# One more of a feed-forward's weight blocks by seven products instead of eight, with its weights loaded earlier

## The chip, the core and the metric

The kernel runs on one core of one Trainium2 chip. The metric is the device time of one execution in microseconds (us). Three runs of the kernel before gave a median of 1127.21 us (1126.88 to 1127.61).

## What is computed

One layer of a streaming encoder for two request groups that share the weights: 512 prompt tokens and 32 sample tokens, 544 columns in all, with 1024 features. The change lies in the first of its three stages, a gated feed-forward with 2816 hidden features:

```python
def swiglu(h, w_gate, w_up, w_down):
    a = jnp.einsum('btd,df->btf', h, w_gate)
    u = jnp.einsum('btd,df->btf', h, w_up)
    return jnp.einsum('btf,fd->btd', jax.nn.silu(a) * u, w_down)

mod = jnp.einsum('bd,de->be', jax.nn.silu(c), w_cond) + b_cond
sh1, sc1, gt1, sh2, sc2, gt2, sh3, sc3, gt3 = jnp.split(mod, 9, axis=-1)
x = post_norm(x, swiglu(modulate(x, sh1, sc1), f1_gate, f1_up, f1_down), 1.0 + gt1, 0.5, ln1_g, ln1_b)
```

The later stages (retention and sparse attention, output projection, second feed-forward) need the other parts of `mod`.

## The kernel before, in words

The 544 columns are worked in two halves of 272. The 22 blocks `f` of 128 hidden features each need a gate and an up product: weight 1024x128 times activation `h` of 1024x272, for both halves.

Every fp32 operand is split into a high and a low float32r part, and a product of 128x128 by 272 columns is three matmuls: high by high, high by low, low by high. So a gate or up product of one half is 24 matmuls, and an ordinary block (`ffn_mm`) is 4 x 24 = 96.

Blocks `f` in the range `SEVEN[0]` go another way (`feed`, `seven`), by a Strassen-like scheme: gate/up and the two halves of the features and of the columns make a 2x2 by 2x2 product, done with seven products of 12 matmuls, 84 in all. For this the kernel needs

- sums of activations, tiles `hs` (`sums[0..7]`), made once by `activation_sums`. For each of k = 0..3, VectorE makes two tiles `la` and `lb` out of `h[k]` and `h[4+k]` (two additions and four subtractions), ScalarE casts them to the high part of `hs`, and VectorE subtracts for the low part. `la` and `lb` are scratch tiles with four buffers in all (`scr`, `bufs=4`).
- sums of raw weights (`weight_sums`: four VectorE operations in place on the raw tiles `wr_g` and `wr_u`), which `split_sums` then splits: ScalarE casts the high part of `wh_s`, VectorE subtracts for the low part.
- the plain gate weights `wh_g` and half of the up weights `wh_u`, split in another way (`negated`): ScalarE casts the high part and writes its negative in the place of the low part, and GpSimd issues a DMA that adds the raw weights from memory to it. The same is done with the ordinary blocks' `wh_w` (`split_w`).

In a block, `seven` has TensorE work in this order: `pC` with `wh_g`, `pA` with `wh_s` and `hs` (the sums 4 to 7), `pB` with `wh_s` and `hs` (the sums 0 to 3), `pA` again, the next block's first `pA`, and so on. ScalarE copies intermediate `pA` out (`snapshot`).

The order of TensorE's instructions is fixed by the program order (`ordered("pe", ...)`), and so is that of SyncE's loads (`ordered("load", ...)`); GpSimd's DMAs all go into one queue. The rest of each engine's order is set by a scheduler, which `pin` holds to program order for the marked instructions. Each engine executes its instructions in order.

Beside this run the modulation pieces (`cond`): 40 loads of 512 KB of `w_cond`, each with two VectorE operations (`ca`), paced by a tick per group of products (a list of gaps).

Of the kernel before, what the change touches and what calls it, by code (L numbers as in the profile page):

```python
# [9 lines left out]
F32 = mybir.dt.float32  # L10
# [21 lines left out]
SEGS = ((((0, HT), 0),), (((HT, TP), 0), ((TP, T), 1)))  # L32
DOWN_G = ((0, 8), (8, 15), (15, 22))
AHEAD = 3
SEVEN = ((5, 17), (4, NF - 1))
WHOLE = (2, 8)


# [1 line left out]
def encoder_layer_kernel(ctx, tc, xT, cT, wc1, w_e, w_cond, b_condT, lnp, w_gu1, w_dn1, w_in, w_out, w_gu2, w_dn2,  # L40
# [51 lines left out]
    def spawn(job):  # L92
        resume(job, now[0] + 1)
# [26 lines left out]
    def fetch_w(src, n, name):  # L120
        raw = wr.tile([P, ND, P], F32, name=f"wr_{name}", tag="wr")
        load(raw[:, :n, :], src)
        return raw
# [37 lines left out]
    def ensure(n):  # L161
        while len(split) < n and stream and stream[0]:
            if not fetched:
                fetch_ahead()
            src, cnt, kw = stream.pop(0)
            split.append(split_w(fetched.pop(0), cnt, "w", src=src, **kw))
# [5 lines left out]
    def queue_w(src, n=ND, **kw):  # L172
        stream.append((src, n, kw))
# [254 lines left out]

    queue_ffn(w_gu1, w_dn1, True)
    for c in range(4):  # L430
        queue_w(w_in[c], lo_eng=nc.gpsimd if c else nc.vector, pool=up)
    for c in [4] + [17 + hh + 4 * j for hh in range(4) for j in range(3)] + [
            5 + c + 4 * j for c in range(4) for j in range(3)] + [29, 30, 31, 32]:
        queue_w(w_in[c], lo_eng=nc.vector if c in (4, 17) else None)
# [103 lines left out]
    for n in range(len(ACC)):  # L538
        catch_up(n, ND)
    ensure(AHEAD)  # L540
    onesr = const.tile([P, P], FR, name="onesr")
    nc.vector.tensor_scalar(onesr, ones, 2.0, None, op0=ALU.mult)

# [22 lines left out]
    def cond(parts, gaps):  # L566
        todo = [(m, d) for m in parts for d in range(ND)]
        ws, accs = [], {}

        def fetch():  # L570
            if len(ws) < len(todo):
                m, d = todo[len(ws)]
                ws.append(up.tile([P, 1024], F32, name=f"wc{m}_{d}", tag="u"))
                load(ws[-1], w_cond[d * P:(d + 1) * P, 1024 * m:1024 * m + 1024])

        fetch()
        yield 1
        fetch()
        yield 2
        for n, (m, d) in enumerate(todo):  # L580
            if d == 0:
                accs[m] = [up.tile([P, 1024], F32, name=f"ca{m}_{r}", tag="u") for r in range(2)]
            fetch()
            for r, acc in enumerate(accs[m]):
                c = cz[:, d, r:r + 1]
                if d == 0:
                    got = nc.vector.tensor_scalar(acc, ws[n], c, None, op0=ALU.mult)
                else:
                    got = nc.vector.scalar_tensor_tensor(acc, ws[n], c, acc, op0=ALU.mult, op1=ALU.add)  # L589
                tc.add_manual_dep(got.ins, last["pe"], NOSYNC, reason="pace")  # L590
            if d == ND - 1:
                spawn(cond_done(m, accs[m]))
            yield gaps[n % len(gaps)]
# [46 lines left out]
    def later(n, job):  # L640
        yield n
        yield from job
# [13 lines left out]
    def activation_sums(h, sums, pace=False):  # L656
        yield 1 if pace else 0
        for k in range(4):
            ta, tb = sums[k], sums[4 + k]
            la, lb = scr("la"), scr("lb")  # L660
            for x, l in ((h[k], la), (h[4 + k], lb)):
                r = nc.vector.tensor_tensor(l, x[:, 0].bitcast(F32), x[:, 1].bitcast(F32), op=ALU.add)
                if pace:
                    tc.add_manual_dep(r.ins, last["pe"], NOSYNC, reason="pace")
            for o, p, q in ((la[:, 0:HT], la[:, HT:T], la[:, 0:HT]), (la[:, HT:T], lb[:, HT:T], la[:, HT:T]),
                            (lb[:, HT:T], lb[:, HT:T], la[:, 0:HT]), (lb[:, 0:HT], lb[:, 0:HT], lb[:, HT:T])):
                nc.vector.tensor_tensor(o, p, q, op=ALU.subtract)
            for x, l in ((ta, la), (tb, lb)):
                nc.scalar.copy(x[:, 0], l)
                nc.vector.tensor_tensor(x[:, 1], l, x[:, 0].bitcast(F32), op=ALU.subtract)  # L670
            yield 2

    def split_hid(dst, src, n):
        if n == 1:
# [1 line left out]
        else:  # L676
            nc.vector.tensor_tensor(dst[:, 1], src, dst[:, 0].bitcast(F32), op=ALU.subtract)

    def feed(h, hid, sums, flat, begun, gu, blocks, whole, lead=None):
        pin = tc.keep_in_program_order  # L680
        LO, HI = slice(0, 4), slice(4, 8)
        raw_g, raw_u, Wg, Wu, Wg2, Wu2 = {}, {}, {}, {}, {}, {}

        def load_gate(f):
            raw_g[f] = fetch_w(gu[f, 0], ND, "g")

        def load_up(f):
            raw_u[f] = up.tile([P, ND, P], F32, name="wr_u", tag="u")
            load(raw_u[f], gu[f, 1])

# [34 lines left out]
        def snapshot(ps, name):  # L725
            s = half_scr(name)
            pin(nc.scalar.copy(s, ps))  # L727
            return s
# [33 lines left out]
        def seven(f):  # L762
            t, u = scr("tnh", [P, 2, HT]), scr("up", [P, 2, HT])
            more = f < last7
            if f + 2 <= last7:
                make_gate(f + 2)
            else:
                ensure(len(split) + 1)
            if f + 3 <= last7:
                load_gate(f + 3)  # L770
            else:
                fetch_ahead()
            if f + 2 <= last7:
                load_up(f + 2)
            C = bank("l", "pC")[:, :HT]
            product(C, Wg[f], 4, h, 4, 0, True, True)
            pin(nc.vector.tensor_tensor(u[:, 0], s1.pop(f), C, op=ALU.add))
            finish_block(0)
            pin(nc.scalar.activation(t[:, 0], u[:, 0], AF.Silu))
            if more:  # L780
                make_up(f + 1, 0)
            tick()
            product(A[f], Wg2[f], 0, sums, 4, 1, False, True)
            s2 = snapshot(A[f], "s2")
            if more:
                weight_sums(f + 1)
                make_up(f + 1, 1)
            finish_block(1)
            B = bank("t", "pB")[:, :HT]
            product(B, Wu2[f], 0, sums, 0, 1, True, True)  # L790
            tick()
            product(A[f], Wu2[f], 4, sums, 0, 0, False, True)
            s4 = snapshot(A[f], "s4")
            pin(nc.vector.tensor_tensor(u[:, 1], s4, B, op=ALU.add))
            if more:
                begin(f + 1)
                split_sums(f + 1, Wg2, raw_g)
                s1[f + 1] = snapshot(A[f + 1], "s1")
            else:
                (lead or first_down)()  # L800
            finish_block(2)
            tick()
            product(A[f], Wg2[f], 4, h, 4, 1, False, True)
            if more:
                split_sums(f + 1, Wu2, raw_u)
            pin(nc.scalar.activation(t[:, 1], A.pop(f), AF.Silu))
            product(B, Wu[f], 0, sums, 4, 0, False, True)
            pin(nc.vector.tensor_tensor(u[:, 0], s2, B, op=ALU.add))
            pending.append((t, u, f))
            if not more:  # L810
                finish_block(0)
            tick()
# [10 lines left out]
        for f in range(2, first7):  # L823
            place(f)
            if f == first7 - 2:
                load_gate(first7)
                load_up(first7)
            if f == first7 - 1:
                load_gate(first7 + 1)
                load_up(first7 + 1)  # L830
                load_gate(first7 + 2)
            st = [None, None], {}
            for which in range(2):
                for i in range(2):
                    ffn_mm(st, h, which, i)
                    if f == first7 - 2 and which == 0:
                        if i == 0:
                            make_gate(first7)
                        else:
                            make_up(first7, 0)  # L840
                            make_up(first7, 1)
                    if f == first7 - 1:
                        if which == 0 and i == 0:
                            make_gate(first7 + 1)
                        if which == 0 and i == 1:
                            weight_sums(first7)
                        if which == 1 and i == 0:
                            split_sums(first7, Wg2, raw_g)
                            split_sums(first7, Wu2, raw_u)
            for i in range(2):  # L850
                ffn_act(st, hid[f] if f < whole else None, i, flat.get(f))
# [13 lines left out]
        for i in range(2):  # L865
            ffn_act(sts[f], hid[f], i)
    flat, following = {}, ([None, None], {})
    spawn(later(4, cond((2, 3, 4, 5, 6), [3] * 4 + [4] * 3 + [6] + [4] * 6 + [4, 3] + [2] * 24)))
    feed(h, hid, sums, flat, None, w_gu1, SEVEN[0], WHOLE[0], lambda: ffn_mm(following, h, 0, 0))
    hid.extend([None] * len(flat))  # L870

    def split_flat():
# [817 lines left out]
```

## Time and profile before

| | us |
|---|---|
| median of three runs | 1127.21 |
| the profiled execution | 1126.96 |
| its span | 1125.2 |
| TensorE busy | 1106.3 (98%) |
| VectorE busy | 855.2 (76%) |
| ScalarE busy | 638.4 (57%) |
| GpSimd busy | 196.0 (17%) |

The profile gives for each engine when an instruction was busy, and for an idle stretch what ended it. TensorE is busy in nearly the whole span: the first blocks of the feed-forward (`gu`) start at 46.65 us, the seven-product blocks run from 82.6 us to 224 us, and the down projection (`dn`) from 269 us to 404 us. A DMA's time is read from its issue to its landing.

### The profile page before, as it was taken

The page shows a single profiled execution, that of the slowest core. Times are in us where ns is not written, and L with a number is a line of the kernel's source. Part 1 is how long each engine was busy: PE and PEld are TensorE (multiplying, and loading weights), DVE is VectorE, ACT ScalarE, POOL GpSimd, SP SyncE. Part 2 cuts the span into 40 slices and gives each one's busy share as a digit, 9 for nine tenths or more (in the row PEclk, how much of TensorE's full clock was granted, in tenths as well). Part 3 has the DMA queues.
Part 4 walks back from the last instruction along what each step waited for, and adds up shares of the span by engine and source line. Part 5 has one row for each costly group of instructions (what it writes and reads, how often), then busy time and mean ns, then how long its engine had stood idle before and what let it go on. Part 6 is the DMA issues. An engine that isn't in the chain of part 4 may idle for free.

```text
span 1125.2 us, 22775 instructions
## 1 busy us (share of the span) xinstructions
PE 1106.3 (98%) x9047; PEld 1075.8 (96%) x9047; DVE 855.2 (76%) x1774; ACT 638.4 (57%) x1121; POOL 196.0 (17%) x217
## 2 busy tenths in 40 slices
PE   8999999999999999999999999999999999999995
PEld 7999999999999999889999899999999999999994
DVE  5778898788868799797899777798798966810416
ACT  3646656754234355865566678656666666653523
POOL 0111111122101303422210101100111111151100
PEclk9999999999999999999999999999999999999998
DMA  9789878996977556644956588843888677578842
GB/s 358 272 237 249 227 191 228 256 259 243 334 201 185 129 218 171 145 118 124 276 112 215 109 269 232 201 172 57 238 212 215 179 187 161 160 205 178 176 73 80
DMA packets 71164, 220.92 MB, mean 196 GB/s; under 512 B 8624, under 2 KB 12848, under 8 KB 71056
## 3 DMA queue, kind: packets, MB, share of 16 engines
q1 hardware_dynamic: 49456, 151.02, 38.2%
q0 software_dynamic: 21456, 68.30, 33.8%
q8 instruction: 71, 1.16, 0.4%
q14 instruction: 37, 0.30, 0.1%
q10 hardware_dynamic: 144, 0.14, 0.0%
HBM read 207.82 MB, written 9.58 MB: 193 GB/s over the span
## 4 chain that ended last, share of the span: by engine, by line
PE 87%; DVE 6%; DMA 4%; ACT 1%; issue 1%; SPq 0%; DVEq 0%; POOL 0%; POOLq 0%; ACTq 0%
PE dn L77 26%; PE in L77 16%; PE pA L77 15%; PE gu L77 10%; PE pB L77 8%; PE pC L77 4%; DMA we_raw<-in_w_e 3%; PE gu_e L77 2%; PE pt L80 1%; PE po L77 1%; PE lg L77 1%; DMA wh_w<-in_w_dn 1%; PE isc L77 1%; PE ro L77 1%; DVE m L1126 1%
## 5 line engine op out<-in xcount | busy, mean ns | idle before, releaser
L77 PE MATMUL dn<-hid,wh_w 128*128 128x272 f32 x2112 | 267.1, 288 | 0.3 <-DMA wh_w<-in_w_dn 0.3
L77 PEld LDWEIGHTS dn<-hid,wh_w 128*128 128x128 f32 x2112 | 265.5, 188 | 0.7 <-DMA wh_w<-in_w_dn 0.5
L77 PE MATMUL in<-h,wh_w 128*128 128x272 f32 x1392 | 186.7, 291 | 0.0
L77 PEld LDWEIGHTS in<-h,wh_w 128*128 128x128 f32 x1392 | 176.6, 188 | 4.9 <-issue 2.9
L131 ACT CAST wh_w<-wr_w 128x1024 fp32r<-128x1024 f32 (+1 forms) x100 | 100.9, 1014 | 99.9 <-PE dn L77 86.5
L77 PE MATMUL gu<-h,wh_w 128*128 128x272 f32 x864 | 109.1, 288 | 0.0
L77 PEld LDWEIGHTS gu<-h,wh_w 128*128 128x128 f32 x864 | 108.5, 188 | 0.0
L589 DVE SCALAR_TENSOR_TENSOR ca<-wc,cz,ca 128x1024 f32<-128x1024 f32 x84 | 107.4, 1298 | 0.0
L77 PE MATMUL pA<-hs,wh_s 128*128 128x272 f32 x744 | 103.7, 288 | 0.7 <-ACT s L727 0.6
L77 PEld LDWEIGHTS pA<-hs,wh_s 128*128 128x128 f32 x744 | 96.8, 188 | 1.1 <-ACT s L727 1.1
L138 ACT ACTIVATE wh_w<-wh_w 128x1024 fp32r<-128x1024 f32 (+1 forms) x78 | 79.5, 1022 | 1.5
L286 DVE SCALAR_TENSOR_TENSOR xs<-dn,C,xs 128x272 f32<-128x272 f32 (+2 forms) x24 | 9.0, 403 | 81.6 <-PE dn L77 81.6
L693 POOL DMA_DIRECT2D wh_g<-in_w_gu x31 | 27.0, 871 | 250.0 <-ACT wh_g L692 172.6
L727 ACT COPY s<-pA 128x272 f32<-128x272 f32 x93 | 35.5, 382 | 58.5 <-PE pA L77 57.9
L139 POOL DMA_DIRECT2D wh_w<-in_w_dn x32 | 28.1, 879 | 174.9 <-ACT wh_w L138 141.6
L716 DVE TENSOR_TENSOR wh_s<-wr_g,wh_s 128x1024 fp32r<-128x1024 f32 x31 | 38.0, 1224 | 20.2 <-ACT wh_s L715 20.2
L77 PE MATMUL pA<-h,wh_g 128*128 128x272 f32 x372 | 51.8, 288 | 0.0
L77 PE MATMUL pB<-hs,wh_u 128*128 128x272 f32 x372 | 51.5, 287 | 0.0
L77 PE MATMUL pC<-h,wh_g 128*128 128x272 f32 x372 | 51.5, 287 | 0.0
L77 PE MATMUL pB<-hs,wh_s 128*128 128x272 f32 x372 | 51.4, 287 | 0.0
L77 PE MATMUL pA<-h,wh_s 128*128 128x272 f32 x372 | 51.4, 287 | 0.0
L77 PEld LDWEIGHTS pA<-h,wh_g 128*128 128x128 f32 x372 | 48.7, 188 | 0.0
(331 smaller groups left out, 2048.4 us busy)
## 6 DMA issues: line engine op xcount, KB each, us to landing
wc<-in_w_cond SPq DMA_DIRECT2D x52, 512.0 KB, 6.6
wr_w<-in_w_in SPq DMA_DIRECT2D x33, 512.0 KB, 5.4
wr_g<-in_w_gu SPq DMA_DIRECT2D x31, 512.0 KB, 3.7
wr_u<-in_w_gu SPq DMA_DIRECT2D x31, 512.0 KB, 4.5
wh_g<-in_w_gu POOLq DMA_DIRECT2D x31, 512.0 KB, 6.7
wr_w<-in_w_dn SPq DMA_DIRECT2D x32, 448.0 KB, 4.3
wh_w<-in_w_in POOLq DMA_DIRECT2D x27, 512.0 KB, 6.4
wh_w<-in_w_dn POOLq DMA_DIRECT2D x26, 448.0 KB, 6.7
```

The lines of the kernel that those rows point to most:

```text
L77: ordered("pe", nc.tensor.matmul(*a, **kw))
L80: ordered("pe", nc.tensor.transpose(*a))
L131: c = nc.scalar.copy(hi[:, :n, :], raw[:, :n, :])
L138: nc.scalar.mul(lo[:, :n, :], hi[:, :n, :].bitcast(F32), -1.0)
L139: nc.gpsimd.dma_start(lo[:, :n, :], src, accum_op=ALU.add)
L286: nc.vector.scalar_tensor_tensor(x[:, sa:sb], ps[:, sa - a:sb - a], coef[r][:, d:d + 1], x[:, sa:sb], op0=ALU.mult, op1=ALU.add)
L589: got = nc.vector.scalar_tensor_tensor(acc, ws[n], c, acc, op0=ALU.mult, op1=ALU.add)
L693: nc.gpsimd.dma_start(lo, src, accum_op=ALU.add)
L716: pin(nc.vector.tensor_tensor(W[f][:, 1], raw[f], W[f][:, 0].bitcast(F32), op=ALU.subtract))
L727: pin(nc.scalar.copy(s, ps))
L1126: behind(behind(nc.vector.max(m8, w), "pe"), "norm")
```

## The change

- `SEVEN[0]` begins at block 4 instead of 5: fourteen blocks go by seven products, and only blocks 2 and 3 stand as ordinary ones ahead of them.
- The raw gate and up weights of block 4 are loaded ahead of the blocks, right behind the first three weight loads, into tiles of the pool `up`.
- `activation_sums` yields one tick instead of two between its four parts, and for k = 0 and 1 makes the low part of `hs` by a negation on ScalarE and an adding DMA of GpSimd, which reads `la` or `lb`, instead of by VectorE.
- The modulation pieces start five ticks later (`later(9, ...)`), and some of their later gaps are one tick instead of two.
- In `seven`, the first `Silu` stands behind the copy `s2` and the second product instead of ahead of them.
- The second gate of the range is made one product later (`which == 1`).
- Three weights of the input projection, used at about 404 us, have their low part made by negation and an adding DMA instead of by a GpSimd subtraction.

```diff
-SEVEN = ((5, 17), (4, NF - 1))
+SEVEN = ((4, 17), (4, NF - 1))
...
-        queue_w(w_in[c], lo_eng=nc.gpsimd if c else nc.vector, pool=up)
+        queue_w(w_in[c], lo_eng=None if c else nc.vector, pool=up)
...
     ensure(AHEAD)
+    first_raw = ({}, {})
+    for which in range(2):
+        raw = up.tile([P, ND, P], F32, name=("wr_g", "wr_u")[which], tag="u")
+        load(raw, w_gu1[SEVEN[0][0], which])
+        first_raw[which][SEVEN[0][0]] = raw
...
                 nc.scalar.copy(x[:, 0], l)
-                nc.vector.tensor_tensor(x[:, 1], l, x[:, 0].bitcast(F32), op=ALU.subtract)
-            yield 2
+                if pace and k < 2:
+                    nc.scalar.mul(x[:, 1], x[:, 0].bitcast(F32), -1.0)
+                    nc.gpsimd.dma_start(x[:, 1], l, accum_op=ALU.add)
+                else:
+                    nc.vector.tensor_tensor(x[:, 1], l, x[:, 0].bitcast(F32), op=ALU.subtract)
+            yield 1 if pace else 2
...
             finish_block(0)
-            pin(nc.scalar.activation(t[:, 0], u[:, 0], AF.Silu))
             if more:
                 make_up(f + 1, 0)
             tick()
             product(A[f], Wg2[f], 0, sums, 4, 1, False, True)
             s2 = snapshot(A[f], "s2")
+            pin(nc.scalar.activation(t[:, 0], u[:, 0], AF.Silu))
...
-                        if which == 0 and i == 0:
+                        if which == 1 and i == 0:
                             make_gate(first7 + 1)
...
-    spawn(later(4, cond((2, 3, 4, 5, 6), [3] * 4 + [4] * 3 + [6] + [4] * 6 + [4, 3] + [2] * 24)))
-    feed(h, hid, sums, flat, None, w_gu1, SEVEN[0], WHOLE[0], lambda: ffn_mm(following, h, 0, 0))
+    spawn(later(9, cond((2, 3, 4, 5, 6), [3] * 4 + [4] * 3 + [6] + [4] * 6 + [4, 3] + [2] * 10 + [2, 1] * 5 + [2] * 4)))
+    feed(h, hid, sums, flat, None, w_gu1, SEVEN[0], WHOLE[0], lambda: ffn_mm(following, h, 0, 0),
+         first_raw)
```

The first place is GpSimd's queue at the start of the feed-forward. `wh_w` are low parts of ordinary blocks, `wh_g` and `wh_u` those of seven-product blocks, and the wait of a row is the semaphore of another engine or of a DMA. Before, behind the subtraction:

```order
L141 TENSOR_TENSOR wh_w<-wr_w,wh_w 128x1024 [waits DMAHW4_49,Activation_49]
L139 DMA wh_w<-in_w_gu 128x1024 [waits Activation_49] x3
L139 DMA wh_w<-in_w_gu 128x1024 [waits PE_49,Activation_49,Pool_49]
L693 DMA wh_g<-in_w_gu 128x1024 [waits DVE_49,PE_49,Activation_49]
L693 DMA wh_u<-in_w_gu 128x512 [waits DMAHW1_49,Activation_49]
```

The same place in the changed kernel:

```order
L141 TENSOR_TENSOR wh_w<-wr_w,wh_w 128x1024 [waits DMAHW4_49,Activation_49]
L139 DMA wh_w<-in_w_gu 128x1024 [waits Activation_49] x2
L708 DMA wh_g<-in_w_gu 128x1024 [waits Activation_49]
L677 DMA hs<-la 128x544 [waits DVE_49,PE_49,Activation_49]
L677 DMA hs<-lb 128x544 [waits DVE_49,DMAHW5_49,PE_49,Activation_49]
L708 DMA wh_u<-in_w_gu 128x512 [waits DMAHW0_49,PE_49,Activation_49]
L677 DMA hs<-la 128x544 [waits DVE_49,DMAHW1_49,PE_49,Activation_49]
L677 DMA hs<-lb 128x544 [waits DMAHW2_49,DMAHW6_49,DVE_49,Activation_49]
```

Three adding DMAs of 512 KB stand first in both kernels. Behind them the queue now holds four adding DMAs of `hs` with 128x544 elements (272 KB) and, between them, one of 256 KB for `wh_u`. The semaphores of GpSimd's DMAs go round eight numbers in this order, so the first `hs<-la` is DMASW3, the first `hs<-lb` DMASW4 and the second `hs<-la` DMASW6.

The second place is VectorE at the sums of k = 2 and k = 3 (`h_2`, `h_6` and `h_3`, `h_7`), where `flat` is the activation of block 2 and `gu` its products. Before:

```order
L662 TENSOR_TENSOR la<-h_2_94 128x544
L662 TENSOR_TENSOR lb<-h_6_98 128x544
L667 TENSOR_TENSOR la<-la 128x272 [waits DVE_49]
L667 TENSOR_TENSOR la<-lb,la 128x272 [waits DVE_49]
L667 TENSOR_TENSOR lb<-lb,la 128x272 [waits DVE_49]
L667 TENSOR_TENSOR lb<-lb 128x272 [waits DVE_49]
L670 TENSOR_TENSOR hs<-la,hs 128x544 [waits DMAHW4_49,Activation_49]
```

In the changed kernel:

```order
L667 TENSOR_TENSOR la<-h_2_94 128x544 [waits DMASW3_49,Activation_49]
L672 TENSOR_TENSOR la<-la 128x272 [waits DVE_49]
L667 TENSOR_TENSOR lb<-h_6_98 128x544 [waits DMASW4_49,Activation_49]
L672 TENSOR_TENSOR la<-lb,la 128x272 [waits DVE_49]
L672 TENSOR_TENSOR lb<-lb,la 128x272 [waits DVE_49]
L672 TENSOR_TENSOR lb<-lb 128x272 [waits DVE_49]
L679 TENSOR_TENSOR hs<-la,hs 128x544 [waits DMAHW4_49,Activation_49]
L203 TENSOR_TENSOR flat<-tnh,gu_0_777 128x272 [waits DMAHW0_49,PE_49]
L679 TENSOR_TENSOR hs<-lb,hs 128x544 [waits Activation_49]
L203 TENSOR_TENSOR flat<-tnh,gu_1_816 128x272 [waits PE_49]
L667 TENSOR_TENSOR la<-h_3_95 128x544 [waits DMASW6_49]
L667 TENSOR_TENSOR lb<-h_7_99 128x544 [waits DVE_49]
```

The third `la` and `lb` now wait for the first two adding DMAs of `hs`, whose source buffers they overwrite, and the fourth `la` waits for the third of those DMAs. Before, none of these rows waited for a DMA of GpSimd.

The third place is VectorE between those sums and the first seven-product block, 4 (`wr_g` and `wr_u` are its raw weights, `gu` the up products of block 3, `pC` the block's own product), in the changed kernel:

```order
L679 TENSOR_TENSOR hs<-lb,hs 128x544 [waits DMAHW4_49,Activation_49]
L726 TENSOR_TENSOR wr_u<-wr_u 128x512 [waits DMAHW0_49]
L203 TENSOR_TENSOR flat<-tnh,gu_0_931 128x272 [waits PE_49]
L726 TENSOR_TENSOR wr_u<-wr_g,wr_u 128x512 [waits DMAHW7_49,DVE_49]
L726 TENSOR_TENSOR wr_g<-wr_u,wr_g 128x512 [waits DVE_49,Pool_49]
L726 TENSOR_TENSOR wr_g<-wr_g 128x512 [waits DVE_49]
L203 TENSOR_TENSOR flat<-tnh,gu_1_966 128x272 [waits PE_49]
L731 TENSOR_TENSOR wh_s<-wr_g,wh_s 128x1024 [waits Activation_49]
L731 TENSOR_TENSOR wh_s<-wr_u,wh_s 128x1024 [waits DMASW0_49,Activation_49]
L792 TENSOR_TENSOR up<-s_1010,pC 128x272 [waits DMASW7_49,PE_49,Activation_49]
```

The corresponding rows before, ahead of block 5, with the pieces of the modulation (`ca`) among them:

```order
L711 TENSOR_TENSOR wr_u<-wr_g,wr_u 128x512 [waits DMAHW1_49]
L587 TENSOR_SCALAR ca_0_983<-wc_0_872,cz 128x1024 [waits DMAHW4_49,DMAHW0_49]
L670 TENSOR_TENSOR hs<-lb,hs 128x544 [waits Activation_49]
L587 TENSOR_SCALAR ca_1_984<-wc_0_872,cz 128x1024
L711 TENSOR_TENSOR wr_g<-wr_u,wr_g 128x512 [waits DVE_49]
L711 TENSOR_TENSOR wr_g<-wr_g 128x512 [waits DVE_49]
```

The pieces of the modulation are gone from this stretch; the weight sums of the first seven-product block stand right behind the last sum of activations.

More of the change, by code (lines that the diff above doesn't have):

```diff
@@ L677, in split_hid, with feed @@
             nc.vector.tensor_tensor(dst[:, 1], src, dst[:, 0].bitcast(F32), op=ALU.subtract)
-    def feed(h, hid, sums, flat, begun, gu, blocks, whole, lead=None):
+    def feed(h, hid, sums, flat, begun, gu, blocks, whole, lead=None, first_raw=({}, {})):
         pin = tc.keep_in_program_order
@@ L682, in feed @@
         raw_g, raw_u, Wg, Wu, Wg2, Wu2 = {}, {}, {}, {}, {}, {}
+        raw_g.update(first_raw[0])
+        raw_u.update(first_raw[1])
         def load_gate(f):
-            raw_g[f] = fetch_w(gu[f, 0], ND, "g")
+            if f not in raw_g:
+                raw_g[f] = fetch_w(gu[f, 0], ND, "g")
         def load_up(f):
+            if f in raw_u:
+                return
             raw_u[f] = up.tile([P, ND, P], F32, name="wr_u", tag="u")
```

## The prediction

> **What bounds the kernel now.** First the page's busy times and the table of who waited for whom on TensorE (us in total, times, longest), for what TensorE has to do and what it waits for.
>
> ```profile
> PE 1106.3 (98%) x9047; PEld 1075.8 (96%) x9047; DVE 855.2 (76%) x1774; ACT 638.4 (57%) x1121; POOL 196.0 (17%) x217
> PE pA L77 <- ACT s L727: 0.6, 1, 0.6
> PE dn L77 <- DMA wh_w<-in_w_dn: 0.3, 1, 0.3
> ```
>
> TensorE works in 98% of the span. In the change's stages it waits only 0.6 us for a ScalarE copy and 0.3 us for a weight. So a matmul less is time less, and any new wait of TensorE is time more. The chain of waits (start, us, what) prices a product: the three ordinary blocks, and 12 matmuls of `pA`.
>
> ```profile
> 46.65 36.08 PE gu L77 x288
> 82.73 1.52 PE pA L77 x12
> ```
>
> 36.08 / 288 = 0.1253 us per matmul; a product of 24 takes 3.01 us, one of 12 takes 1.50.
>
> **One block by seven products.** It saves 96 - 84 = 12 matmuls, 1.5 us on TensorE, which sets the end. The rest of the question is whether what the first seven-product block needs is there a block earlier. With two ordinary blocks ahead, TensorE reaches block 4 at 46.65 + 8 x 3.01 = 70.7 us; after the first `pA` and `pC` it wants `wh_s` and `hs` at 73.7, and the low part of `wh_s`, by the third matmul, at 73.95. Nothing ahead of 46.65 moves: the early raw loads stand behind the loads that these blocks start with, and the DMA engines are idle then. Of the busy time by stretches the last two columns are the share of the 16 DMA engines and the GB/s:
>
> ```profile
> 40.00:44.00 4.00, 3.96 (x31) 3.63 (x30) 2.46 (x5) 3.88 (x6) 2.23 (x1) 1.00 0.03 12
> 46.00:65.00 19.00, 19.00 (x154) 19.00 (x153) 14.80 (x31) 9.91 (x20) 2.76 (x3) 1.00 1.01 292
> ```
>
> From 46 to 65 us, however, the DMA engines are full, and now the sums of activations go through them. Two of the four leave VectorE in favour of adding DMAs, in one queue behind the three adding DMAs of weights. GpSimd's timeline (start, us) shows when those three were issued, and the DMA tables of the stretches 46 to 51, 51 to 53 and 53 to 55 how long each took to land:
>
> ```profile
> 46.58 1.02 POOL L139 DMA_DIRECT2D wh_w<-in_w_gu  x1 [2.39 <-ACT hid L206]
> 51.84 0.87 POOL L139 DMA_DIRECT2D wh_w<-in_w_gu  x1 [4.24 <-ACT wh_w L138]
> 54.00 0.86 POOL L139 DMA_DIRECT2D wh_w<-in_w_gu  x1 [1.29 <-ACT tnh L201]
> wh_w<-in_w_gu POOLq DMA_DIRECT2D x1, 512.0 KB, 10.1
> wh_w<-in_w_gu POOLq DMA_DIRECT2D x1, 512.0 KB, 8.7
> wh_w<-in_w_gu POOLq DMA_DIRECT2D x1, 512.0 KB, 11.3
> ```
>
> They landed at 56.7, 60.5 and 65.3: one per 3.8 to 4.8 us, one behind the other. The changed queue has the same three first, and beside them SyncE still loads weights, only two fewer (those moved ahead), so I keep 65.3 for the third. The first `hs<-la` cannot land before it, though ScalarE casts the first sum already at about 54:
>
> ```profile
> 53.88 0.64 ACT L669 CAST hs<-la 128x544 fp32r<-128x544 f32 x1
> ```
>
> What one of 272 KB takes no row shows. The upper end is 272/512 of the mean spacing above, 4.3 us: 2.3. For the lower, GpSimd's rows of a 512 KB DMA with a 256 KB one behind it, and their tables (86 to 88, 88 to 89):
>
> ```profile
> 87.11 0.88 POOL L693 DMA_DIRECT2D wh_g<-in_w_gu x1 [6.71 <-ACT tnh L779]
> 88.75 0.87 POOL L693 DMA_DIRECT2D wh_u<-in_w_gu x1 [0.75 <-ACT wh_u L692]
> wh_g<-in_w_gu POOLq DMA_DIRECT2D x1, 512.0 KB, 6.8
> wh_u<-in_w_gu POOLq DMA_DIRECT2D x1, 256.0 KB, 6.4
> ```
>
> Landings at 93.9 and 95.15, 1.25 us apart, so 1.3 for 272 KB. I take the middle, 1.85. Then `la` of k = 0 lands at 67.15, `lb` at 69.0, and behind `wh_u` `la` of k = 1 at 72.7.
>
> VectorE, which executes in order, cannot start the third `la` before the first has landed (its buffer), nor the third `lb` before the second. Queued behind these are all sums of k = 2 and 3, the four weight sums and the low part of `wh_s`, for which TensorE waits. Their durations, from VectorE's timeline of k = 1 (two additions, four subtractions, the low parts, `flat`), of a block's weight sums, and of the low part of `wh_s`; and ScalarE's cast ahead of the latter:
>
> ```profile
> 55.84 0.72 DVE L662 TENSOR_TENSOR la<-h 128x544 f32<-128x544 f32 x1
> 57.11 0.43 DVE L667 TENSOR_TENSOR la<-la 128x272 f32<-128x272 f32 x1
> 58.89 0.72 DVE L670 TENSOR_TENSOR hs<-la,hs 128x544 fp32r<-128x544 f32 x1
> 59.52 0.43 DVE L203 TENSOR_TENSOR flat<-tnh,gu 128x272 f32<-128x272 f32 x1
> 59.87 0.72 DVE L670 TENSOR_TENSOR hs<-lb,hs 128x544 fp32r<-128x544 f32 x1
> 99.80 0.69 DVE L711 TENSOR_TENSOR wr_u<-wr_u 128x512 f32<-128x512 f32 x1
> 102.64 0.43 DVE L794 TENSOR_TENSOR up<-s,pB 128x272 f32<-128x272 f32 x1
> 84.33 1.22 DVE L716 TENSOR_TENSOR wh_s<-wr_u,wh_s 128x1024 fp32r<-128x1024 f32 x1
> 79.09 1.04 ACT L715 CAST wh_s<-wr_g 128x1024 fp32r<-128x1024 f32 x1
> ```
>
> From the landing of `lb` to the start of the fourth `la`: an addition 0.63, three subtractions of 0.475, two low parts of 0.63 and two `flat` of 0.35, with 0.1 for the wait: 4.1 us, so 73.1, 0.4 after its own buffer came free. From there: two additions and four subtractions 3.05, two low parts 1.28, the four weight sums 2.84 with one `flat` 0.35 between them, the cast 1.04, the low part 1.22, 0.2 for two handovers: 10.0 us. The low part of `wh_s` is there at 83.1, wanted at 73.95: **TensorE waits 9.1 us**. By the ends 1.3 and 2.3 the fourth `la` starts at 72.1 or 74.6, and the wait is 8.2 or 10.7.
>
> Such a wait costs more than itself. The clock slows when TensorE stands still: its last matmul before the end of the kernel, and the granted clock (third column from the right) behind it; and at the kernel's start the same matmul cold and warm:
>
> ```profile
> 1111.37 0.62 PE L77 MATMUL pv<-sq,cm 128*128 128x272 f32 x2
> 1112.00:1114.00 2.00, 0.00 (x0) 0.00 (x0) 1.89 (x4) 0.68 (x2) 1.67 (x2) 1.00 0.00 0
> 1116.00:1118.00 2.00, 0.00 (x0) 0.00 (x0) 1.91 (x4) 0.70 (x2) 0.00 (x0) 0.50 0.00 0
> 1.23 3.78 PE L77 MATMUL idle<-zeros 128*128 128x256 f32 x8 [1.23 <-POOL zeros L496]
> 7.48 2.76 PE L77 MATMUL idle<-zeros 128*128 128x256 f32 x12
> ```
>
> Between 2 and 6 us after the last matmul the clock is at half, and eight cold matmuls took 3.78 us where warm ones take 8 x 0.23: 1.9 us lost. After a pause of 8 us I expect the same loss, +1.9; its ends are 0 and twice that. The Trainium skill, "TensorE: Matmul & The Clock Gate", section "What's actually happening", has the clock at half after an idle window of about 3.4 us and until a busy one of the same length; by that the loss would be an estimated 1.7 us instead, and the rows agree with the rule. It speaks against this change.
>
> Once through, I expect no second wait: the up weights' `wh_s` follow 1.2 us later, TensorE has 1.5 us of work until then, and each later block brings VectorE its usual work within 10.5 us, without the pieces of the modulation for now.
>
> **The other edits.** The `Silu` behind the copy `s2`: the copy no longer waits in ScalarE's queue for VectorE's sum, so the 0.6 us goes (0 to -0.6; what the `Silu` feeds is wanted a block later). The four negations are ScalarE's, which has room in the 46 to 65 row. The pieces of the modulation start later but end at the same tick, so five of them move towards the down projection, where TensorE hides them (in 46 to 404 us it waits only for the two above); were that cover gone, a piece's two operations cost 2.5 us of VectorE. The input projection's three low parts free GpSimd, where a subtraction stood ahead of the late weight:
>
> ```profile
> 375.00 3.44 POOL L141 TENSOR_TENSOR wu_w<-wr_w,wu_w 128x1024 fp32r<-128x1024 f32 x1 [1.31 <-ACT wu_w L131]
> 378.38 0.88 POOL L139 DMA_DIRECT2D wh_w<-in_w_dn  x1
> ```
>
> That weight's DMA now comes ahead of them: -0.3 (to 0).
>
> **The sum**, against the profiled execution, 1126.96 us (span 1125.2, 1.76 around it; 0.25 under the median): 1126.96 - 1.5 - 0.6 - 0.3 + 9.1 + 1.9 = **1135.6**. With the bounds above its own range is 1132.8 (wait 8.2, no cold clock) to 1140 (wait 10.7, twice the cold loss, the two small gains at nothing).
>
> **Rivals.**
> *The sums come in time: faster.* The first `hs<-la` is ready to be issued at about 55.3. If GpSimd's queue were drained by then, each transfer would land soon after issue, the fourth `la` would start by 63 and `wh_s` be ready by 73. Then nothing stands against the savings: 1126.96 - 2.4 = 1124.6. Against it are the three rows that landed up to 65.3; for it only that two loads move into the idle stretch ahead of 46. It decides from the point at which the first `hs<-la` lands before about 58. 10%. The Trainium skill, "DMA: Bandwidth & Descriptors", section "Anatomy of one DMA", fits an adding queue's transfer by 2.0 us and its bytes at 436 GB/s; that would be an estimated 2.6 us for these 272 KB and would carry this rival. The rows of 10.1, 8.7 and 11.3 us for 512 KB do not agree.
>
> *A shorter wait.* With fewer loads beside them the three land up to 3 us earlier, at 62.3, and the following at 1.3 spacing: `lb` at 64.9, the fourth `la` at 69, `wh_s` at 79, a wait of 5.1, and 1126.96 - 2.4 + 5.1 + 1.9 = 1131.6; between this and the first rival lies all that ends at no change. 15%, 6 of them within 0.2%.
>
> *A longer wait.* If a DMA out of on-chip memory is paid by the row and not by the byte, each `hs` costs 4.3 like 512 KB: the second `la` lands at 65.3 + 3 x 4.3 + 2.2 = 80.4, the wait is 16.5 and the time 1143. No row shows such a source. 7%.
>
> **The numbers.** The forecast has 68%. 0.2% of the time, 2.3 us, is about what a measurement of this kernel can tell from no change. Faster: the first rival, 10%. Same: 6%. Slower: 68 + 9 + 7 = 84%. The range leaves out the first rival, the part at no change and most of the longest wait: 1129.5 to 1140.
>
> **What would show it.** In the changed profile: TensorE idle for about 9 us at 74 us, ahead of `pA<-hs,wh_s`, released by VectorE's `wh_s`; GpSimd's `hs` DMAs issued from 55 and landing after more than 8 us; VectorE idle ahead of the third `la`, released by a DMA; the granted clock under 1 in that slice; 192 matmuls `gu` ahead of the blocks. I am wrong if the first `hs<-la` lands before 60, or if TensorE runs through 74 us.

## The result, and the profile after

| | before | after |
|---|---|---|
| median of the runs, us | 1127.30 (1126.88 to 1127.61, 4 runs) | 1137.58 (1136.63 to 1138.71, 4 runs) |
| profiled execution, us | 1126.96, span 1125.2 | 1138.71, span 1136.9 |
| matmuls on TensorE | 9047 | 9035 |

The ratio is 1.0091 [1.0078, 1.0104]: the changed kernel is slower by 10.3 us (8.8 to 11.7). The page's busy times and the table of who waited for whom on TensorE (us in total, times, longest), of the changed kernel:

```profile
PE 1108.6 (98%) x9035; PEld 1076.8 (95%) x9035; DVE 855.4 (75%) x1778; ACT 647.1 (57%) x1133; POOL 190.5 (17%) x221
...
PE pA L77 <- ACT s L742: 9.1, 1, 9.1
PE pC L77 <- DVE flat L203: 0.4, 1, 0.4
```

The twelve matmuls are gone, yet TensorE is busy for 2.3 us more: some matmuls ran slower. And there is one new wait of 9.1 us. TensorE's timeline (start, us, what, and in brackets the idle time before it with what ended it) shows where:

```profile
73.52 1.77 PE L77 MATMUL pC<-h,wh_g 128*128 128x272 f32 x12 [0.41 <-DVE flat L203]
84.36 3.09 PE L77 MATMUL pA<-hs,wh_s 128*128 128x272 f32 x12 [9.08 <-ACT s L742]
87.25 2.92 PE L77 MATMUL pB<-hs,wh_s 128*128 128x272 f32 x12
89.97 1.83 PE L77 MATMUL pA<-hs,wh_s 128*128 128x272 f32 x12
91.64 1.68 PE L77 MATMUL pA<-h,wh_g 128*128 128x272 f32 x12
```

TensorE ends `pC` at 75.3 and stands until 84.36, ahead of the first product with `hs` and `wh_s`. Then it is slow: the 36 matmuls from 84.36 to 91.64 took 7.28 us, where 36 x 0.1253 is 4.51. So 2.8 us more are lost behind the wait. The busy times by stretches name the reason in their third column from the right, the granted clock:

```profile
78.00:80.00 2.00, 0.00 (x0) 0.00 (x0) 1.92 (x5) 1.97 (x3) 0.00 (x0) 1.00 0.00 0
80.00:82.00 2.00, 0.00 (x0) 0.00 (x0) 1.86 (x4) 0.21 (x1) 0.88 (x1) 0.52 0.00 0
...
88.00:90.00 2.00, 2.00 (x11) 2.00 (x11) 1.69 (x3) 0.72 (x2) 0.86 (x1) 0.50 0.91 143
90.00:92.00 2.00, 2.00 (x16) 2.00 (x16) 0.00 (x0) 0.16 (x1) 0.00 (x0) 0.92 1.03 193
```

The clock is full for almost 5 us after the last matmul, then at half from 80 to a little past 90, nearly 6 us into the new work.

Whom TensorE waits for is read backwards. On GpSimd, the four adding DMAs of `hs` (start of the issue, us), and their landing from the DMA tables of the stretches 57 to 58, 61 to 62, 68 to 69 and 70 to 71 (KB, us from issue to landing):

```profile
57.50 0.89 POOL L677 DMA_DIRECT2D hs<-la  x1 [2.79 <-ACT hs L674]
61.27 0.88 POOL L677 DMA_DIRECT2D hs<-lb  x1 [2.87 <-DMA wr_g<-in_w_gu]
...
68.65 0.86 POOL L677 DMA_DIRECT2D hs<-la  x1 [1.41 <-PE gu L77]
70.55 0.88 POOL L677 DMA_DIRECT2D hs<-lb  x1 [1.04 <-DVE la L672]
```

```profile
hs<-la POOLq DMA_DIRECT2D x1, 272.0 KB, 10.9
hs<-lb POOLq DMA_DIRECT2D x1, 272.0 KB, 9.0
hs<-la POOLq DMA_DIRECT2D x1, 272.0 KB, 4.3
hs<-lb POOLq DMA_DIRECT2D x1, 272.0 KB, 3.7
```

They land at 68.4, 70.3, 72.95 and 74.25. VectorE's timeline has the matching starts:

```profile
68.49 0.73 DVE L667 TENSOR_TENSOR la<-h 128x544 f32<-128x544 f32 x1 [11.48 <-DMA hs<-la]
...
70.33 0.72 DVE L667 TENSOR_TENSOR lb<-h 128x544 f32<-128x544 f32 x1 [0.63 <-DMA hs<-lb]
...
74.36 0.72 DVE L667 TENSOR_TENSOR la<-h 128x544 f32<-128x544 f32 x1
...
83.11 1.23 DVE L731 TENSOR_TENSOR wh_s<-wr_g,wh_s 128x1024 fp32r<-128x1024 f32 x1 [0.77 <-ACT wh_s L730]
```

VectorE stands for 11.48 us, and the two rows behind start 0.1 us after the first two landings: it waited for the buffers `la` and `lb`, which the DMAs were still reading. All its later work is queued behind, to the low part of `wh_s`, which ends at 84.34. The wait of TensorE, however, is put down to ScalarE's copy of `pA` (L742). ScalarE's timeline says why:

```profile
82.04 1.04 ACT L730 CAST wh_s<-wr_g 128x1024 fp32r<-128x1024 f32 x1 [1.83 <-DVE wr_g L726]
82.99 1.04 ACT L730 CAST wh_s<-wr_u 128x1024 fp32r<-128x1024 f32 x1
83.93 0.38 ACT L742 COPY s<-pA 128x272 f32<-128x272 f32 x1
```

The copy stands behind two casts of `wh_s`, and these wait for VectorE's weight sums. It ends at 84.31, the low part at 84.34: two releasers of one chain, and the profile names the one that it takes for the last.

### The profile page after: what moved, and what is told of

It reads as the page before. It is cut to its first block, busy times and chain, and to the rows that moved or that the text cites. A ratio compares the mean times of both kernels' runs of the same rounds, so it can differ in the third digit from the quotient of the medians.

```text
span 1136.9 us, 22776 instructions
## 1 busy us (share of the span) xinstructions
PE 1108.6 (98%) x9035; PEld 1076.8 (95%) x9035; DVE 855.4 (75%) x1778; ACT 647.1 (57%) x1133; POOL 190.5 (17%) x221
## 4 chain that ended last, share of the span: by engine, by line
PE 83%; DVE 6%; DMA 6%; ACT 2%; issue 1%; SPq 0%; DVEq 0%; POOL 0%; ACTq 0%; POOLq 0%
PE dn L77 24%; PE pA L77 17%; PE in L77 15%; PE pB L77 9%; PE gu L77 7%; PE pC L77 4%; DMA we_raw<-in_w_e 3%; PE gu_e L77 2%; DMA wr_w<-in_w_gu 1%; PE pt L80 1%; DMA wr_w<-in_w_in 1%; DMA hs<-lb 1%; PE po L77 1%; PE isc L77 1%; PE lg L77 1%
## 5 line engine op out<-in xcount | busy, mean ns | idle before, releaser
L77 PE MATMUL pA<-hs,wh_s 128*128 128x272 f32 x768 | 108.4, 291 | 9.1 <-ACT s L742 9.1
L77 PEld LDWEIGHTS pA<-hs,wh_s 128*128 128x128 f32 x768 | 101.5, 191 | 9.4 <-ACT s L742 9.3
L77 PE MATMUL gu<-h,wh_w 128*128 128x272 f32 x768 | 96.8, 288 | 0.0
L77 PEld LDWEIGHTS gu<-h,wh_w 128*128 128x128 f32 x768 | 96.4, 188 | 0.0
L742 ACT COPY s<-pA 128x272 f32<-128x272 f32 x96 | 36.9, 384 | 92.3 <-PE pA L77 92.0
L77 PE MATMUL pB<-hs,wh_s 128*128 128x272 f32 x384 | 54.3, 292 | 0.0
L77 PEld LDWEIGHTS pB<-hs,wh_s 128*128 128x128 f32 x384 | 51.2, 192 | 0.0
```

What stands on the lines that cost most here:

```text
L77: ordered("pe", nc.tensor.matmul(*a, **kw))
```

## The experiments

Each kernel was timed beside the kernel before on the same chip (median before 1127.29 for e1 to e4 without e3b, 1127.68 for e3b and e5 to e7, 1127.67 for e8). The theory is that of the prediction: VectorE waits for the buffers that the adding DMAs read. The rivals are that the sums themselves come late through the DMAs, whatever the buffers, and that the wait lies in what the change took away or moved elsewhere. The brackets behind a ratio are its interval.

**e1: all sums on VectorE.** Undoes the activations' adding DMAs alone.

```diff
-                if pace and k < 2:
+                if False:
```

> The changed kernel with one part undone: VectorE makes the low parts of the sums for all four k, and GpSimd's four adding DMAs of hs are gone. Theory (the sums' adding DMAs stand behind three of the weights, and VectorE waits for their source buffers): VectorE no longer waits 11.5 us ahead of the third la; from 50.8 us it works 17.8 us on the sums, 1.1 on flat, 2.8 on weight sums, takes up the first sum with pC, and the low part of wh_s is there about 1.6 us after TensorE wants it. Wait at pA<-hs,wh_s 1 to 2 us instead of 9.1, no slow clock: 1126 to 1127.5 us. Rival (the chain of VectorE and ScalarE is too long for two ordinary blocks in any case, the DMAs only stand beside it): a wait of 6 us or more, and 1133 us or more.

Measured 1126.09 us, 0.9988 [0.9979, 0.9997]. The waits of TensorE:

```profile
PE pA L77 <- DVE wh_s L731: 0.8, 1, 0.8
...
PE pA L77 <- ACT wh_s L730: 0.4, 1, 0.4
```

With four subtractions more on VectorE, and no DMA to wait for, 9.1 us of wait become 1.2. The adding DMAs carry the loss; the block taken a step earlier, the early loads and the moved pieces carry 1.2 us of the wait at most.

**e2: DMAs as in the changed kernel, with buffers of their own.** The first two pairs of sums lie in buffers that no later sum overwrites.

```diff
-            la, lb = scr("la"), scr("lb")
+            la, lb = (unit("la")[:, 0], unit("lb")[:, 0]) if pace and k < 2 else (scr("la"), scr("lb"))
```

> The changed kernel with its adding DMAs of hs, in the same place of the queue, but la and lb of k = 0 and 1 get buffers of their own, so that VectorE does not wait for the DMAs to have read them. Theory: the DMAs land as late as before (68 to 74.5 us), just in time for pA and pB at 75 us; VectorE runs through from 51 us and has the low part of wh_s at about 75 us; the wait of 9.1 us and the slow clock behind it go, and the saving of one block is left: 1124.9 us (1124.4 to 1125.8). Rival (what counts is that the sums themselves land late, not the buffers): TensorE still waits some us for hs, 1128 us or more.

Measured 1125.20 us, 0.9981 [0.9972, 0.999]. TensorE's product, VectorE's low part of `wh_s`, and the first adding DMA of a sum (in the table of 57 to 58):

```profile
75.17 1.76 PE L77 MATMUL pA<-hs,wh_s 128*128 128x272 f32 x12 [0.54 <-ACT s L742]
```

```profile
73.92 1.23 DVE L731 TENSOR_TENSOR wh_s<-wr_g,wh_s 128x1024 fp32r<-128x1024 f32 x1 [1.12 <-ACT wh_s L730]
```

```profile
hs<-la POOLq DMA_DIRECT2D x1, 272.0 KB, 11.4
```

Issued at 57.09, that DMA lands at 68.5, as late as in the changed kernel, and the last at 74.4. But the low part of `wh_s` ends at 75.15 and not at 84.34. So the late landing of `hs` costs nothing here, since all four are there before `pC` ends at 74.6, though the last only by 0.2 us; the buffer held until the landing costs all of it. This is the experiment that tells theory and rival apart.

**e4: a shorter queue.** Two of the three 512 KB adding DMAs ahead of the first `hs` become subtractions on GpSimd. The buffers stay shared.

```diff
-                    eng = (nc.gpsimd, nc.vector)[which] if f == 2 and first else None
+                    eng = ((nc.gpsimd, nc.vector)[which] if f == 2 else nc.gpsimd if f == 3 else None) if first else None
```

> The changed kernel with block 3's two low parts made by a GpSimd subtraction instead of by adding DMAs, so that one adding DMA instead of three stands ahead of the sums; loads and everything else as they were. Theory (place in GpSimd's queue): the first hs<-la lands at about 62 us instead of 68.4, VectorE's chain ends about 6 us earlier, the wait is about 3 us with little or no slow clock: 1129.5 us (1128 to 1131). Rival (the loads of SyncE beside them fill the DMA engines, and each adding DMA takes its 9 to 12 us whatever stands ahead): the first hs<-la lands at about 66.5 us, the wait shrinks by 2 us at most: 1135 us or more.

Measured 1133.55 us, 1.0057 [1.0044, 1.0069]. VectorE's third `la` and TensorE's product:

```profile
65.68 0.73 DVE L667 TENSOR_TENSOR la<-h 128x544 f32<-128x544 f32 x1 [7.23 <-DMA hs<-la]
```

```profile
80.94 3.09 PE L77 MATMUL pA<-hs,wh_s 128*128 128x272 f32 x12 [7.28 <-ACT s L742]
...
87.33 1.67 PE L77 MATMUL pA<-h,wh_g 128*128 128x272 f32 x12
```

The ordinary blocks start at 46.43 here and at 47.38 in the changed kernel's profile. Counted from there, the first `hs` lands 1.9 us earlier (65.5 for 68.4), and TensorE starts 2.5 us earlier (80.94 for 84.36). That the landing sets TensorE's start is borne out again. Of the cause of the late landing the run decides less: neither number came. The place in the queue is worth some 2 us; with only one DMA ahead the `hs` still took 9.4 us, at a time when the weight loads fill the DMA engines. How the rest divides between these loads and that one DMA this run leaves open; e7 shows that the loads have a part. The 36 matmuls behind the wait took 6.39 us here (80.94 to 87.33), 1.9 more than 4.51, where the changed kernel lost 2.8.

**e3 and e3b: the cold clock alone.** TensorE multiplies zeros while it waits, which only adds work that nothing reads: 34 matmuls in e3, 18 in e3b. The wait itself stays.

```diff
+            if begun is None and f == first7:
+                warm = bank("o", "warm")
+                for _ in range(34):
+                    mm(warm[:, 0:256], zeros[:, 0, 0:P], zeros[:, 0, 0:256], start=True, stop=True)
             product(A[f], Wg2[f], 0, sums, 4, 1, False, True)
```

> The changed kernel with 34 matmuls of zeros by zeros, whose result nothing reads, on TensorE just ahead of the product that waits 9.1 us; at 0.23 us each they fill 7.8 us of the wait. Theory (the three products behind the wait take 3.09, 2.92 and 1.83 us because the clock has fallen to half): the wait by others' work stays, the clock stays at 1.00 and the three products take 1.5 us each: 2.8 us less, 1134.8 us. Rival (these products are slow because they wait for the next weights and copies, which are late too): no change, 1137.5 us.

Measured 1139.32 us, 1.0108 [1.0095, 1.0122]; a miss. One such matmul stands in the trace as two records and took 0.43 us, so that the 34 outlasted the wait:

```profile
74.72 14.84 PE L77 MATMUL warm<-zeros 128*128 128x256 f32 x68
```

With 18 in place of 34:

> As e3_warm, with 18 matmuls of zeros instead of 34: there each took 0.43 us and together they outlasted the wait (14.8 us where it is 9.1), so that it showed full speed behind them but no gain. 18 take 7.8 us and end about 1.5 us before the low part of wh_s is there. Theory (half clock behind the pause): the pause that is left is too short for the clock to fall, the three products behind it take 1.5 us each as in e3_warm, and the kernel takes 2.8 us less than the changed one: 1134.8 us. Rival (the products wait for something that is late with them): 1137.5 us.

Measured 1134.83 us, 1.0063 [1.0051, 1.0075]. TensorE's timeline:

```profile
74.94 7.93 PE L77 MATMUL warm<-zeros 128*128 128x256 f32 x36
84.11 1.77 PE L77 MATMUL pA<-hs,wh_s 128*128 128x272 f32 x12 [1.23 <-ACT s L742]
...
88.72 1.67 PE L77 MATMUL pA<-h,wh_g 128*128 128x272 f32 x12
```

The products start at 84.11, no earlier than without the zeros (counted from the start of the ordinary blocks even 0.8 later, as `pC` waited longer here), but the 36 matmuls take 4.61 us (84.11 to 88.72) and not 7.28. The kernel is 2.8 us faster (1137.58 - 1134.83), 3.2 by the two ratios. The granted clock stays at 1.00 from 70 to 95 us here. So the loss behind the wait is the clock, and it is 2.7 to 2.8 us.

**e5: the kernel before with the `Silu` moved.** One edit of the change alone.

```diff
-            pin(nc.scalar.activation(t[:, 0], u[:, 0], AF.Silu))
             if more:
                 make_up(f + 1, 0)
             tick()
             product(A[f], Wg2[f], 0, sums, 4, 1, False, True)
             s2 = snapshot(A[f], "s2")
+            pin(nc.scalar.activation(t[:, 0], u[:, 0], AF.Silu))
```

> The kernel before with one part of the change alone: the first Silu of a seven-product block behind the copy s2. Theory: the copy no longer stands behind the Silu's wait for VectorE, TensorE's wait of 0.6 us at pA goes and nothing comes instead: 0.6 us less, 1126.7 us. Rival (the Silu now comes late for what it feeds, or the copy then waits for the next thing in ScalarE's queue): 1127.3 us or more.

Measured 1125.17 us, 0.9985 [0.9976, 0.9994]: -1.7 us (-2.7 to -0.7), more than expected. TensorE's timeline of one seven-product block, in the kernel before and in e5:

```profile
108.47 1.66 PE L77 MATMUL pB<-hs,wh_s 128*128 128x272 f32 x12
110.69 1.76 PE L77 MATMUL pA<-hs,wh_s 128*128 128x272 f32 x12 [0.57 <-ACT s L727]
112.29 1.66 PE L77 MATMUL pA<-h,wh_g 128*128 128x272 f32 x12
```

```profile
108.19 1.66 PE L77 MATMUL pB<-hs,wh_s 128*128 128x272 f32 x12
...
111.19 1.67 PE L77 MATMUL pA<-h,wh_g 128*128 128x272 f32 x12
```

Two products of 12 take 112.29 - 108.47 = 3.82 us up to the next one before, and 3.00 in e5: 0.8 are gone here, of which the profile lists 0.57 as a wait. The block before it had 3.36 (97.60 to 100.96), without any listed wait, against 3.01. From the start of the ordinary blocks to 159 us e5 needs 1.4 us less than before. Gaps too short to be listed made the difference. Up to the input projection e5 needs 2.1 us less; the other 0.7 lies in the down projection (134.05 us for 134.80), where the listed wait of 0.3 us is gone.

**e6: e2 with the old schedule of the modulation's pieces.**

```diff
-    spawn(later(9, cond((2, 3, 4, 5, 6), [3] * 4 + [4] * 3 + [6] + [4] * 6 + [4, 3] + [2] * 10 + [2, 1] * 5 + [2] * 4)))
+    spawn(later(4, cond((2, 3, 4, 5, 6), [3] * 4 + [4] * 3 + [6] + [4] * 6 + [4, 3] + [2] * 24)))
```

> e2_own_bufs (1125.2 us) with the modulation pieces on their old schedule. Theory: two operations of a piece (0.74 us each) stand again among the weight sums that TensorE waits for, and three more loads fill the DMA engines beside the adding DMAs, so that wh_s and the last hs come 1.5 to 3 us later: 1126.7 to 1128.2 us. Rival (the pieces were covered there, as VectorE waits for products of TensorE anyway): 1125.2 us.

Measured 1129.92 us, 1.0021 [1.0011, 1.0031]. The waits of TensorE:

```profile
PE dn L77 <- DMA wh_w<-in_w_dn: 2.6, 1, 2.6
...
PE pA L77 <- DVE wh_s L731: 0.7, 1, 0.7
...
PE pA L77 <- ACT wh_s L730: 0.7, 1, 0.7
```

The 1.4 us at `pA` were expected, in place of e2's 0.5: a piece stands among the weight sums. The 2.6 us at the down projection were not. GpSimd's timeline there, of e6, and TensorE's behind the wait:

```profile
376.90 0.86 POOL L139 DMA_DIRECT2D wu_w<-in_w_in  x1 [2.88 <-ACT wu_w L138]
377.74 0.93 POOL L139 DMA_DIRECT2D wh_w<-in_w_dn  x1
```

```profile
388.33 5.67 PE L77 MATMUL dn<-hid,wh_w 128*128 128x272 f32 x31 [2.57 <-DMA wh_w<-in_w_dn]
```

A low part of the input projection, wanted after 400 us, is issued ahead of a weight that TensorE wants at about 386 us. In e2 the order is the other way round (376.68 for this weight, 380.26 for the low part), and there is no wait. In e6 the weight was issued 1.1 us later, as ScalarE's negations stand in the same order (the weight's ends at 377.34), and took 10.6 us to land instead of 8.5. That what stands ahead in the queue made the landing longer fits, but no run tests it here. The order of issue hangs on a schedule that moves other work.

The wait of 2.6 us costs more than itself too. The 31 matmuls behind it took 5.5 us up to the next work, where the kernel before took 4.0 for the same 31: the granted clock stood at half from 389.4 to 392.9 us. With these 1.5 us the parts come to 5.0 (0.9 more at `pA`, 2.6, 1.5); by the two ratios e6 is 4.5 us slower than e2.

**e7: e2 without the early raw loads.** The loads ahead are taken out; the block loads its own.

```diff
-    for which in range(2):
-        raw = up.tile([P, ND, P], F32, name=("wr_g", "wr_u")[which], tag="u")
-        load(raw, w_gu1[SEVEN[0][0], which])
-        first_raw[which][SEVEN[0][0]] = raw
```

> e2_own_bufs (1125.2 us) without the early loads of block 4's raw weights: they come at their ordinary place, at about 45 us, ahead of the last ordinary weight. Theory: the idle stretch of the DMA engines at 40 to 44 us stays unused, that weight lands 2 us later, and with it every adding DMA behind it; the last hs land 2 to 3 us after TensorE wants them: 1127 to 1128.5 us. Rival (the DMAs of hs stand in GpSimd's queue, which is not full of loads, and land as before): 1125.2 us.

Measured 1125.59 us, 0.9986 [0.9977, 0.9995], against e2's 0.9981 [0.9972, 0.999]; a miss. One wait appears and another goes:

```profile
PE pA L77 <- DVE wh_s L727: 1.1, 1, 1.1
```

It is 1.1 us in place of e2's 0.5. By the ratios the two differ by 0.6 us, which these runs do not tell from nothing. The step that failed is the landing: the first `hs`, issued at 58.58, took 6.7 us where e2's took 11.4, and counted from the start of the ordinary blocks it landed 2.2 us earlier, not later. The same three adding DMAs of 512 KB stand ahead of it, but beside it SyncE loads less: from 62 to 66 us the DMA engines moved 179 GB/s, 277 in e2. So the loads beside an adding DMA have a part in how long it takes, and not its place in the queue alone.

**e8: e2 with the copy first.** What is left in e2 is the copy of `pA` behind the casts of `wh_s`. The second cast and its low part go behind the copy.

```diff
-                            split_sums(first7, Wu2, raw_u)
...
         s1[first7] = snapshot(A[first7], "s1")
+        split_sums(first7, Wu2, raw_u)
```

> e2_own_bufs (1125.2 us) with ScalarE's copy of block 4's first pA ahead of the cast of the second wh_s instead of behind it. Theory: the 0.5 us that TensorE still waits there for that copy goes down to the wait for the low part of the first wh_s, 0 to 0.3 us: 1124.9 us, faster than both kernels, though not to be told from 1125.2. Rival (the second wh_s is then late in turn for pB): 1125.2 us or more, with a wait at pB.

Measured 1124.81 us, 0.9978 [0.9968, 0.9989]. TensorE's timeline:

```profile
74.61 1.51 PE L77 MATMUL pA<-hs,wh_s 128*128 128x272 f32 x10 [0.32 <-DVE wh_s L731]
```

ScalarE's copy is no longer waited for; 0.3 us for the low part is left. It is the fastest of these kernels: 2.5 us (1.2 to 3.6) below the kernel before and 12.8 below the changed one (1137.58 - 1124.81). From e2 it cannot be told apart.

## Why the prediction was right, point by point

- **The mechanism and its chain** were right from the landing on. VectorE waits for buffers (e2), from there the chain has the predicted length: 4.06 us from the landing of `lb` to the fourth `la` (70.3 to 74.36; predicted 4.1), and 9.98 from there to the end of the low part (74.36 to 84.34; predicted 10.0). The wait is 9.08 where 9.1 was forecast.
- **The landings** came at 68.4, 70.3 and 72.95 for the forecast 67.15, 69.0 and 72.7. Of the first difference, 1.25, 0.9 is the whole stage: the ordinary blocks start at 47.38 in this profile, at 46.48 in that of before; e2, which does the same work ahead of them, has 47.39, and e1 and e8 have 46.61 and 46.81, so this is the variation of runs. TensorE's want moved by as much, 0.9 with the stage and 0.4 by a new wait at `pC` that I did not forecast; that the two differences cancel, so that the wait came out at 9.1, is in part luck. One `hs` followed another after 1.9 us (68.4 to 70.3), near the 1.85 chosen. I had said that I would be wrong if the first landed before 60. My reason for the late landing, the three DMAs ahead, one behind the other, is borne out only in part: without two of them the first `hs` lands 1.9 us earlier (e4), not by two spacings of 4.3, and with fewer loads beside them 2.2 us earlier than in e2 (e7).
- **The releaser** was read only half. I named the low part of `wh_s` and overlooked that the copy of `pA` stands behind two casts in ScalarE's queue. Here both end together, so it costs nothing; with the buffers freed it is what is late next (0.5 us in e2, 0.3 of another kind in e8).
- **The cold clock** was mis-sized: 2.8 us, not 1.9. My row was that of matmuls at the kernel's start, called cold by their duration alone (the clock column reads 1.00 there); here the half clock lasted 6.0 us into the new work (84.36 to 90.3). What I missed is that the loss has no one size. By stretches of a quarter us the granted clock was at half from 80.1 to 90.3 us here, from 78.1 to 84.9 in e4 and from 389.4 to 392.9 in e6: 10.2, 6.8 and 3.4 us, three, two and one times 3.4. How much of it falls on work depends on when within such a step the pause begins and ends: 2.8 us were lost here, 1.9 in e4, 1.5 in e6. The Trainium skill, "TensorE: Matmul & The Clock Gate", section "What's actually happening", has a window of 3413 ns and calls it free-running. The traces agree with both. My estimate of 1.7 us let the busy window begin with the work; here it did not.
- **The `Silu`** was mis-sized: I took the listed wait, 0.6 us, as the end of its range. e5 has -1.4 us in the seven-product blocks; the -1.7 (-2.7 to -0.7) of its times holds the down projection's share too.
- **The twelve matmuls** are gone as counted (9035). **No second wait** came: behind 84 us no other stands in the table for this stage.
- **The weight of the down projection** (-0.3): its wait is gone, but also in e5, which has the old order, while e3 and e4, which have the new one, list 0.3 and 0.2 us. That the freed GpSimd ended it is not shown, and it gained nothing: the down projection, from its start (269.31 and 279.71) to that of the input projection, took 134.80 us before and 134.83 after.
- **The pieces**: that they are hidden where they went is right (e2 has no wait there). Their move was not idle, as e6, with the old schedule, is 4.5 us slower than e2.
- **The rival "the sums come in time"** had the right price for a wrong reason: 1124.6 forecast, and e2 and e8 have 1125.20 and 1124.81, with sums that land as late as in the changed kernel. Its condition, a landing before 58, was not the one that decides; a free buffer is.

The 10.3 us go as follows, by stretches of the two profiled executions. TensorE's timeline has the start of the ordinary blocks, of the input projection and of the last down projection; before:

```profile
46.48 3.68 PE L77 MATMUL gu<-h,wh_w 128*128 128x272 f32 x28
...
404.11 3.19 PE L77 MATMUL in<-h,wu_w 128*128 128x272 f32 x24
...
1097.77 12.32 PE L77 MATMUL dn<-hid,wh_w 128*128 128x272 f32 x96
```

After:

```profile
47.38 2.81 PE L77 MATMUL gu<-h,wh_w 128*128 128x272 f32 x21
...
414.54 3.19 PE L77 MATMUL in<-h,wu_w 128*128 128x272 f32 x24
...
1109.55 12.32 PE L77 MATMUL dn<-hid,wh_w 128*128 128x272 f32 x96
```

From the first to the second row it is 357.63 us before and 367.16 after: 9.5 more. The parts: -1.5 (matmuls), -1.4 (`Silu`), 0 (weight), +9.1 and +0.4 (the two new waits), +2.8 (clock), together +9.4; 0.1 is not accounted for. From the second to the third it is 693.66 and 695.01. The change doesn't touch these stages; e2, e4 and e5, with the same work there, took 693.6 to 693.8 and e3b 695.3, so I take the 1.35 as the variation of runs; its cause is not shown. The profiled execution is also the longest of the four. In the forecast, two mis-sizings of 0.8 (`Silu`) and 0.9 us (clock) nearly cancelled, which is luck.

What was not tried: an earlier landing of all four sums with shared buffers, and the new place of the second gate by itself.

## What to carry to other kernels

Where an elementwise step is handed to a DMA, its source buffer is held until the DMA lands: count how many later users of this buffer stand in an in-order engine's queue, and give the handed-over tiles buffers of their own before believing the saving. Here the handed-over result came late without cost, while the held buffer cost 9.1 us of wait, and the clock behind the pause 2.8 more. And a listed wait is no measure of what its removal brings: gaps too short for any row made 1.4 us of a listed 0.6 (e5), and one of 2.6 us cost 1.5 more behind it (e6).

## What the runs showed of the hardware

- An adding DMA of 512 KB beside a full stream of weight loads took 9.3 to 12.3 us to land (three of them, issued from 47 to 54 us in the changed kernel); the tables of 51 to 52 and of 53 to 54.5:

```profile
wh_w<-in_w_gu POOLq DMA_DIRECT2D x1, 512.0 KB, 9.3
wh_g<-in_w_gu POOLq DMA_DIRECT2D x1, 512.0 KB, 12.3
```

- An adding DMA of 272 KB out of on-chip memory took 10.9 and 9.0 us behind and beside such transfers, 6.7 and 5.3 with fewer loads beside (e7), and 4.3 and 3.7 later. The Trainium skill, "DMA: Bandwidth & Descriptors", section "Anatomy of one DMA", has a fit for GpSimd's DMAs, without a word on adding ones, that gives an estimated 2.6 us; no row of these runs agrees.
- GpSimd never had more than three adding DMAs under way in this stretch. In the changed kernel the negation for the first `hs` ended at 55.22, but its DMA was issued at 57.50, 0.2 us after the first of the three ahead of it had landed (57.3). The next followed the second's landing by 0.3 us (61.27 after 61.0), and so on (68.65 after 68.4, 70.55 after 70.3; in e4 61.99, 65.84 and 67.07 after 61.8, 65.5 and 66.9). This is read from the times; the profile names other releasers for these rows. What sets the three isn't shown, nor what it costs.
- After TensorE's last matmul the granted clock stayed full for 4.8 us in the changed kernel (75.3 to 80.1), 4.4 in e4 (73.7 to 78.1) and 2.5 at the end of the kernel before (1112.0 to 1114.5); in e6, behind a pause of 2.6 us, it fell 1.1 us after the work had begun again. It was then at half for 10.2, 6.8 and 3.4 us (changed kernel, e4, e6). In e3b and e7, with pauses of 1.2 and 1.1 us there, it stayed at 1.00.
